# One wide matmul for two narrow ones in a channel mixer, and a new cost in the list schedule

## The chip, the cores and the metric

The kernel runs on one NeuronCore of a Trainium2 chip. The metric is the device time of one execution in microseconds (us); smaller is better.

## The reference

One block of a language model works on 256 tokens of 1024 features. It has a token mixer with three branches (block-sparse attention called NSA, an mLSTM, and cross attention to a memory), a gated merge, an output projection, and then a channel mixer. The channel mixer is the part that the change rewrites:

```python
x = x + rmsnorm(y @ w_out[l], g_post_mix[l])

h = rmsnorm(x, g_pre_ffn[l])
gu = h @ w_ffn_in[l]                       # [256, 1024] @ [1024, 5632]
gate, up = gu[..., :D_FF], gu[..., D_FF:]  # D_FF = 2816
x = x + rmsnorm((jax.nn.silu(gate) * up) @ w_ffn_down[l], g_post_ffn[l])
```

All values are float32.

## The kernel before

**Products in three parts.** TensorE multiplies float32r values here. So that the result is near float32, each float32 array is split into a high part (a ScalarE copy to float32r) and a low part (VectorE: the value less its high part); that is `split`. A product is then three matmuls into one accumulator: high x high, high x low, low x high. `mm3` issues the three, and `fmaj` does so for all eight feature tiles of 128.

**Units.** The weights come as 162 units of 128 x 1024 (512 KB), each by one DMA of SyncE's queue into one of four buffers `raw`. `unit` fetches one and splits it into `whi` (ScalarE) and `wlo` (VectorE), four buffers each.

**Two forms of a product.** `fmaj` and `fpair` keep a block of the weights stationary and move the activations: an accumulator [128 features, 256 tokens], matmuls 256 columns wide. `tmaj` keeps a block of the activations stationary and moves the weights: [128 tokens, 512 features], matmuls 512 wide. The merge gates, the queries and most of the input projection use the first form; the output projection, the first four feature tiles of the channel mixer (`gate0`, `up0`) and the down projection (`scaled`, "ffn_down") the second.

**The channel mixer.** `xh` and `xl` are the high and low part of the activations, feature-major [128, 8, 256]. For the feature tiles i = 4 to 21 a loop makes `fpair` (gate tile and up tile, one unit each, in the two halves of one bank of PSUM), multiplies the gate by 1/rms (`rfb`), applies silu on ScalarE, multiplies by the up half, and splits the result into `us`, the operand of the down projection. `ps_ds` chooses the bank: two of tag "d", then three of tag "s", in turn.

**The order of the work.** The kernel text only records instructions. `Plan.schedule` then makes a list schedule over all engines: every instruction has a cost (`Plan.cost`), latencies between engines are added, and on every engine the ready instruction that comes first in the program is issued. The result is a fixed order on each engine. For TensorE, `op.load` is a least distance between two matmuls (109 ns for float32r), and the cost is the columns at 2.4 per ns and 2 ns. A tag of a pool gets as many buffers as the first request for it says.

Of the kernel before, what the change touches and what calls it, by code (L numbers as in the profile page):

```python
# [18 lines left out]
S = 256          # tokens  # L19
D = 1024  # L20
KD = D // P      # feature tiles of the model dimension
# [11 lines left out]
# columns of w_in  # L33
C_Q, C_KV, C_G, C_ML, C_IF, C_O, C_QM, C_MG = 0, 1024, 2560, 2608, 4144, 4152, 4664, 5176

# columns of the array of constants
K_ID, K_TRI, K_RV, K_BM, K_M0, K_C1, K_MT, K_END = 0, 128, 256, 257, 261, 533, 549, 677
# columns of the array of gains and small weights
# [4 lines left out]
class View:  # L43
    """A part of a tile that has no place yet."""
# [54 lines left out]
    def region(self):  # L99
        """First and last partition, and the elements of a partition as bits."""  # L100
        t = self.tile
        key = repr(self.steps)
        if key not in t.regions:
            p = int(self.ix.flat[0]) // t.n
            bits = np.zeros(t.n, bool)
            bits[self.ix[0].ravel() % t.n] = True
            t.regions[key] = (p, p + self.shape[0], int.from_bytes(np.packbits(bits).tobytes(), "big"))
        return t.regions[key]


class Slot:
    """A tile of the plan: its place is chosen when its first instruction is issued."""
# [50 lines left out]
class Plan:  # L163
    """Records the instructions in program order, with what they read and write, and issues them
    in the order of a list schedule: on every engine the ready one that comes first in the
    program. Tiles of a tag get their buffers in program order."""
# [8 lines left out]
    @contextmanager  # L175
    def later(self, n):
        """The instructions inside come as if n places later in the program."""
        self.boost -= n
        yield
        self.boost += n  # L180
# [46 lines left out]
    @staticmethod  # L227
    def cost(op):
        n = op.outs[0].n if op.outs else 0
        views = op.outs + op.ins  # L230
        sources = [v for v in op.ins if not v.tile.psum and v.n > 1]
        wide = op.method in ("tensor_copy", "tensor_scalar") and not any(v.tile.psum for v in op.outs)
        op.port = op.eng == "POOL" and bool(op.ins) or op.eng == "DVE" and len(sources) > 1 - wide
        if op.eng == "SP":
            return math.prod(views[0].shape) * 4 / 360.0
        if op.eng == "PE":
            dtype = op.a[1].dtype
            op.load = 56.0 if dtype == BF16 else 109.0 if dtype == F32R or op.method == "transpose" else 214.0
            rate = 1.2 if op.method == "transpose" else 0.6 if dtype == F32 else 2.4
            return n / rate + 2  # L240
        n = max(v.n for v in views)
        psum = any(v.tile.psum for v in views)
        pointers = sum(v.n == 1 for v in op.ins)
        if op.eng == "ACT":
            return (50 if psum else 95) + 0.833 * n + 93 * ("accum_out" in op.kw or pointers > 0)
        if op.eng == "DVE":
            fast = not psum and op.method in ("tensor_copy", "tensor_scalar")
            return 67 + (0.52 if fast else 1.04) * n + 60 * pointers
        if op.method == "memset":
            return 40 + 0.8 * n  # L250
        if op.kw.get("op") == ALU.pow:
            return 300 + 165 * n
        if op.method == "tensor_copy":
            return 100 + 3.4 * n
        return 100 + 1.4 * n if op.method == "tensor_scalar" else 150 + 2.1 * n
# [9 lines left out]
    def schedule(self):  # L265
# [10 lines left out]
        def offer(op):  # L276
            """Makes op a candidate if its new tiles can have places; else it waits for the tag."""
            r = op.ready
            for t in op.tiles:
                if t.real is None:  # L280
                    tag = t.tag
                    if tag.next != t.seq or not tag.free:
                        tag.waiting.setdefault(t.seq, []).append(op)
                        return
                    r = max(r, tag.free[0][0])
            avail[op.eng].append((max(r, held(op)), op))

        def held(op):
            """A bank of PSUM serves one engine at a time, and so do the ports that GpSimd shares."""
            ends = [end + self.latency(o, op) for t in op.tiles if t.psum  # L290
                    for e, (o, end) in t.busy.items() if e != op.eng]
            if op.port:
                ends += [end for e, end in port.items() if e != op.eng]
            return max(ends, default=0.0)
# [91 lines left out]
def block_kernel(ctx, tc, order, xN, xT, memT, cst, vec, row, wg, w1, w2, W, out):  # L386
# [75 lines left out]
    def fmaj(out, xs, ks, wu, b0=0, first=True, last=True):  # L462
        """out [128 features, 256] += blocks of a unit (from b0) times the tiles ks of xs."""
        hi, lo = wu
        for i, k in enumerate(ks):
            b = slice((b0 + i) * P, (b0 + i + 1) * P)
            mm3(out, hi[:, b], lo[:, b], xs[0][:, k, :], xs[1][:, k, :],
                first and i == 0, last and i == len(ks) - 1)

    def fpair(xs, w, i, ps_new=ps_d):  # L470
        """[128, 2, 256]: the i-th pair of feature tiles of the weights w."""
        ps = ps_new([P, 2, S])
        for j in range(2):
            fmaj(ps[:, j, :], xs, range(KD), unit((w, 2 * i + j)))
        return ps

    def tmaj(xs, *key, n=4, ps_new=ps_d, into=None, last=0):
        """[128 tokens, 512] for both halves of the tokens, from n units of two feature tiles each; the
        last ones are used for the first half of the tokens before the second."""
# [29 lines left out]
    def warm_up(n):  # L509
        """Products of no use, that bring the tensor engine's clock up while it would wait."""  # L510
# [4 lines left out]
    def colsum(sq):  # L515
        """[128, 2]: per token, the sum of sq [128, 2, 256] over the partitions and the tiles."""
# [7 lines left out]
    def bcast(r, ps):  # L524
        """ps [128, 256]: the column r [128, 2] of the tokens, on every row."""
# [114 lines left out]
    msk = one.tile([P, 416], BF16, name="msk")          # m0 (272), c1 (16), mt (128)  # L640
# [56 lines left out]
    # running sums of logf, and i - sums  # L697
# [34 lines left out]
    # columns: selected keys 128-255, 0-127, compressed keys, window keys 0-127, 128-255  # L732
    kh = bigt("KK", 2, [P, NG, 528], F32R, "kh")
    kl = bigt("KK", 2, [P, NG, 528], F32R, "kl")
# [61 lines left out]
    for h2 in range(2):  # L796
        pvm = ps_v([P, 2, S], "pvm")
        ptm = [[work.tile([P, 2, S], F32R, tag=f"pT{i}", bufs=2, name="pTm") for i in range(2)] for _ in range(2)]
        for tb in range(2):
# [18 lines left out]
            pt = ps_t([P, 2, 2, P], "ptx")          # m tile, head, t  # L818
# [256 lines left out]
    def scaled(name, xs, n, g, z, scale, pre):  # L1075
        """z [128 tokens, 2, 1024]: the products with the units of a name times the gains g and, per token,
        pre; yields per half of the tokens 1/rms of the products times the root of scale."""
# [17 lines left out]
    xh = bigt("KK", 2, [P, KD, S], F32R, "xh")  # L1095
    xl = bigt("KK", 2, [P, KD, S], F32R, "xl")
# [34 lines left out]
    for tb in range(2):  # L1131
# [7 lines left out]
        split(us[0][:, 0, :, t], us[0][:, 1, :, t], pt)  # L1139
    for i in range(4, KF):  # L1140
        ps = fpair((xh, xl), "ffn_in", i, ps_ds)
        sl_ = work.tile([P, S], F32, tag="sq", bufs=3, name="silu")
        DVE.tensor_mul(sl_, ps[:, 0, :], rfb)
        ACT.activation(sl_, sl_, AF.Silu)
        DVE.tensor_mul(sl_, ps[:, 1, :], sl_)
        u = us[i // 4]
        split(u[:, 0, i % 4, :], u[:, 1, i % 4, :], sl_)
# [19 lines left out]
def _layout(inputs):  # L1167
# [10 lines left out]
    def blocks(w, cols, k0=0, k1=None):  # L1178
        """[128, k, cols] of the rows k0..k1 (tiles)."""
# [69 lines left out]
def _stream(units, order):  # L1249
    """The units in the order of their use."""  # L1250
# [27 lines left out]
```

## Time and the profile before

| | |
|---|---|
| median of 3 runs | 562.93 us (562.88 to 563.34) |
| span of the profiled execution, first to last instruction | 561.4 us |
| the median less that span | 1.5 us |
| TensorE matmuls (PE), busy | 551.9 us, 98% |
| TensorE weight loads (PEld), busy | 516.5 us, 92% |
| VectorE (DVE), busy | 404.5 us, 72% |
| ScalarE (ACT), busy | 334.2 us, 60% |
| mean DMA rate | 170 GB/s |

The page gives no separate total time for the profiled execution; its own time is the span and what lies around it. In the page's lines, a group such as `pd<-xh,whi` names the tile that is written, then the tiles that are read; "128x256" is partitions by elements of the moving operand; the numbers after the bar are the group's busy time in us, the mean ns of one instruction from start to end, and the engine's idle time before it. All instructions are recorded in one helper, so all stand at line 382, and groups are told apart by their tiles: in the channel mixer `pd` and `pss` are the banks of tag "d" and "s". A row of a timeline or of the chain begins with its start and its length in us. Matmuls overlap in the array, so the sum of their lengths is more than their share of the time.

### The profile page before, as it was taken

What the parts mean: (1) busy time and instruction counts of PE and PEld (TensorE: products, weight loads), DVE (VectorE), ACT (ScalarE), POOL (GpSimd) and SP (SyncE); (2) the same over time, 40 slices, a digit from 0 to 9 for tenths busy, and PEclk for the clock granted to TensorE, in tenths of its full rate; (3) what the DMA queues carried; (4) which work ended last, traced back from release to release, by engine and by line L of the source; (5) the groups of instructions that cost most, each with busy time, mean ns of one, the idle gap of its engine ahead of it and who ended that gap; (6) DMA issues with size and microseconds to landing.
All of it is one profiled execution on the core that took longest, in us unless ns stands there. A gap on an engine that the chain in (4) does not pass through costs nothing.

```text
span 561.4 us, 10304 instructions
## 1 busy us (share of the span) xinstructions
PE 551.9 (98%) x3964; PEld 516.5 (92%) x3964; DVE 404.5 (72%) x802; ACT 334.2 (60%) x658; POOL 36.0 (6%) x44
## 2 busy tenths in 40 slices
PE   8999999999999999999999999999999999999994
PEld 8899998998989999999999998878999999988883
DVE  4897398598897989987786877865565656654543
ACT  6775677566596858777697444774444444444430
POOL 1110000002002011302111000000000000000000
PEclk9999999999999999999999999999999999999998
DMA  7994327617345253434435655744555545556522
GB/s 246 356 350 154 113 86 228 205 56 238 129 121 180 76 178 124 135 119 160 151 117 158 216 189 188 257 156 123 177 189 183 182 175 179 186 185 191 189 71 75
DMA packets 29281, 95.28 MB, mean 170 GB/s; under 512 B 3376, under 2 KB 6704, under 8 KB 28976
## 3 DMA queue, kind: packets, MB, share of 16 engines
q1 hardware_dynamic: 29232, 94.63, 51.5%
q8 instruction: 31, 0.51, 0.4%
q14 instruction: 18, 0.15, 0.1%
HBM read 92.52 MB, written 1.05 MB: 167 GB/s over the span
## 4 chain that ended last, share of the span: by engine, by line
PE 92%; DMA 3%; ACT 2%; DVE 2%; issue 0%; SPq 0%; DVEq 0%; ACTq 0%
PE pd L382 46%; PE pss L382 23%; PE pnl L382 6%; PE sc L382 3%; PE pvn L382 3%; PE pmm L382 2%; PE ptn L382 2%; DMA memt<-in_memT 2%; PE ph L382 2%; ACT whi L382 1%; DMA raw<-in_W 1%; PE pw L382 1%; PE pn L382 1%; PE pgf L382 1%; PE psm L382 1%; PE pvm L382 1%
## 5 line engine op out<-in xcount | busy, mean ns | idle before, releaser
L382 DVE TENSOR_TENSOR wlo<-raw,whi 128x1024 fp32r<-128x1024 f32 (+1 forms) x161 | 195.4, 1217 | 102.1 <-ACT whi L382 100.7
L382 ACT ACTIVATE whi<-raw 128x1024 fp32r<-128x1024 f32 (+1 forms) x161 | 167.6, 1046 | 164.3 <-issue 72.3
L382 PE MATMUL pd<-hh,whi 128*128 128x256 f32 x416 | 119.7, 288 | 0.3 <-DVE vs L382 0.3
L382 PE MATMUL pd<-hh,wlo 128*128 128x256 f32 x416 | 119.7, 288 | 0.0
L382 PE MATMUL pd<-hl,whi 128*128 128x256 f32 x416 | 119.5, 287 | 0.0
L382 PEld LDWEIGHTS pd<-hh,whi 128*128 128x128 f32 x416 | 79.5, 191 | 0.8 <-DVE vs L382 0.7
L382 PEld LDWEIGHTS pd<-hl,whi 128*128 128x128 f32 x416 | 79.4, 191 | 0.1
L382 PEld LDWEIGHTS pd<-hh,wlo 128*128 128x128 f32 x416 | 79.4, 191 | 0.0
L382 PE MATMUL pss<-xh,wlo 128*128 128x256 f32 x160 | 45.4, 284 | 0.0
L382 PE MATMUL pss<-xl,whi 128*128 128x256 f32 x160 | 45.4, 284 | 0.0
L382 PE MATMUL pss<-xh,whi 128*128 128x256 f32 x160 | 45.4, 283 | 0.0
L382 PE MATMUL pss<-whi,u 128*128 128x512 f32 x132 | 42.4, 392 | 0.0
L382 PE MATMUL pd<-xh,whi 128*128 128x256 f32 x128 | 36.2, 283 | 0.0
L382 PE MATMUL pd<-xl,whi 128*128 128x256 f32 x128 | 36.2, 283 | 0.0
L382 PE MATMUL pd<-xh,wlo 128*128 128x256 f32 x128 | 36.2, 283 | 0.0
L382 PEld LDWEIGHTS pss<-xh,whi 128*128 128x128 f32 x160 | 30.7, 192 | 0.0
L382 PEld LDWEIGHTS pss<-xl,whi 128*128 128x128 f32 x160 | 30.7, 192 | 0.0
L382 PEld LDWEIGHTS pss<-xh,wlo 128*128 128x128 f32 x160 | 30.7, 192 | 0.0
L382 PEld LDWEIGHTS pss<-whi,u 128*128 128x128 f32 x132 | 24.8, 188 | 5.5
L382 ACT ACTIVATE pp<-sc,mx 128x128 f32<-128x128 f32 (+1 forms) x64 | 27.1, 439 | 0.4 <-DVE mx L382 0.3
L382 PE MATMUL pss<-wlo,u 128*128 128x512 f32 x66 | 25.9, 392 | 0.0
L382 DVE TENSOR_REDUCE mx<-sc 128x1 f32<-128x16 f32 (+2 forms) x96 | 22.6, 284 | 3.3 <-PE sc L382 3.0
(306 smaller groups left out, 1243.9 us busy)
## 6 DMA issues: line engine op xcount, KB each, us to landing
raw<-in_W SPq DMA_DIRECT2D x159, 512.0 KB, 3.4
w<-in_w SPq DMA_DIRECT2D x2, 1024.0 KB, 7.0
raw<-in_W SPq DMA_DIRECT2D x6, 256.0 KB, 5.6
xt<-in_xT SPq DMA_DIRECT2D x2, 512.0 KB, 7.6
x<-in_xN SPq DMA_DIRECT2D x2, 512.0 KB, 4.9
out<-z SPq DMA_DIRECT2D x8, 128.0 KB, 2.0
memt<-in_memT SPq DMA_DIRECT2D x6, 128.0 KB, 5.4
wgt<-in_wg SPq DMA_DIRECT2D x1, 512.0 KB, 6.3
```

The source lines that it names most:

```text
L382: op.ins_ = getattr(op.real, op.method)(*map(arg, op.a), **{k: arg(x) for k, x in op.kw.items()})
```

## The change

The high and low activations come to stand side by side in one tile, `xc` [128, 8, 2, 256]. A new function `fcat` multiplies a block of the high weights by both with one matmul 512 wide, into the two halves of a bank, and a block of the low weights by the high activations with one matmul 256 wide, into the first half. A unit thus takes 16 matmuls for 24, with the same number of columns, and a whole bank, where before a pair of units shared one. `joined` adds the two halves: ScalarE copies the second half to a work tile, VectorE adds the first. It asks for six buffers of tag "sq", which has been made with three. `kh` and `kl` of the attention, which had the buffers of `xh` and `xl` before, become the halves of one tile. And `Plan.cost` gives a float32r matmul 13 ns beside its columns instead of 2. The other lines of the diff only drop comments and docstrings; the core of it is:

```diff
-            return n / rate + 2
+            return n / rate + (13 if dtype == F32R and op.method != "transpose" else 2)
...
+    def fcat(xc, w, ps):
+        hi, lo = unit(w)
+        b = lambda k: slice(k * P, (k + 1) * P)
+        for k in range(KD - 1):
+            PE.matmul(ps, hi[:, b(k)], xc[:, k], start=k == 0, stop=False)
+        for k in range(KD):
+            PE.matmul(ps[:, 0, :], lo[:, b(k)], xc[:, k, 0], start=False, stop=False)
+        PE.matmul(ps, hi[:, b(KD - 1)], xc[:, KD - 1], start=False, stop=True)
+        return ps
...
-    kh = bigt("KK", 2, [P, NG, 528], F32R, "kh")
-    kl = bigt("KK", 2, [P, NG, 528], F32R, "kl")
+    kk_ = bigt("KK", 1, [P, 2, NG, 528], F32R, "kk")
+    kh, kl = kk_[:, 0], kk_[:, 1]
...
-    xh = bigt("KK", 2, [P, KD, S], F32R, "xh")
-    xl = bigt("KK", 2, [P, KD, S], F32R, "xl")
+    xc = bigt("KK", 1, [P, KD, 2, S], F32R, "xc")
+    xh, xl = xc[:, :, 0], xc[:, :, 1]
...
+    def joined(ps):
+        t = work.tile([P, S], F32, tag="sq", bufs=6, name="join")
+        ACT.activation(t, ps[:, 1, :], AF.Copy)
+        DVE.tensor_add(t, t, ps[:, 0, :])
+        return t
+
     for i in range(4, KF):
-        ps = fpair((xh, xl), "ffn_in", i, ps_ds)
-        sl_ = work.tile([P, S], F32, tag="sq", bufs=3, name="silu")
-        DVE.tensor_mul(sl_, ps[:, 0, :], rfb)
-        ACT.activation(sl_, sl_, AF.Silu)
-        DVE.tensor_mul(sl_, ps[:, 1, :], sl_)
+        gate = joined(fcat(xc, ("ffn_in", 2 * i), ps_ds([P, 2, S])))
+        DVE.tensor_mul(gate, gate, rfb)
+        ACT.activation(gate, gate, AF.Silu)
+        up = joined(fcat(xc, ("ffn_in", 2 * i + 1), ps_ds([P, 2, S])))
+        DVE.tensor_mul(up, gate, up)
         u = us[i // 4]
-        split(u[:, 0, i % 4, :], u[:, 1, i % 4, :], sl_)
+        split(u[:, 0, i % 4, :], u[:, 1, i % 4, :], up)
```

## The prediction

> **What bounds the kernel now.** I read the page's busy shares first, then the chain that ended last, then TensorE's waits, and then the trace of the channel mixer alone.
>
> ```profile
> span 561.4 us, 10304 instructions
> PE 551.9 (98%) x3964; PEld 516.5 (92%) x3964; DVE 404.5 (72%) x802; ACT 334.2 (60%) x658; POOL 36.0 (6%) x44
> ...
> PEclk9999999999999999999999999999999999999998
> ...
> PE 92%; DMA 3%; ACT 2%; DVE 2%; issue 0%; SPq 0%; DVEq 0%; ACTq 0%
> ...
> 20.00:300.00 280.00, 279.55 (x2148) 265.19 (x2147) 230.84 (x544) 200.39 (x464) 31.62 (x27) 1.00 0.49 160
> ...
> PE warm L382 <- POOL ones L382: 1.0, 1, 1.0
> ...
> PE pd L382 <- ACT xh L382: 0.2, 1, 0.2
> ```
>
> TensorE is the bound: it is busy for 98% of the span at full granted clock, the chain is 92% matmuls, and between 20 and 300 us (columns of the window row: length, then busy time of PE, PEld, DVE, ACT, POOL) it lacks 0.45 us. The six waits listed for it run from 1.0 to 0.2 us. So time is saved only by making TensorE's own instruction stream shorter, and lost by anything that makes it wait. Busy time cannot say how short, because the matmuls overlap in the pipeline; for that I need start-to-start times.
>
> The span is 561.4 us, and the median of the runs shown is 562.93, so 1.5 us lie around the span. I take these as unchanged and subtract from 562.93.
>
> **The removed and added matmuls.** The stage that is changed is 18 pairs of units, 36 units, each of 24 matmuls 256 wide:
>
> ```profile
> L382 PE MATMUL pss<-xh,whi 128*128 128x256 f32 x160 | 45.4, 283 | 0.0
> ...
> L382 PE MATMUL pd<-xh,whi 128*128 128x256 f32 x128 | 36.2, 283 | 0.0
> ```
>
> Two more groups of each count (the products with xl and with wlo) make (160 + 128) x 3 = 864 = 36 x 24. The 283 ns are start to end; the pace is in the chain, whose pieces give start, length and count:
>
> ```profile
> 395.73 11.52 PE pd L382 x96
> 407.25 17.28 PE pss L382 x144
> ...
> 493.65 31.73 PE pss L382 x138
> 543.50 5.44 PE pss L382 x24
> ```
>
> 11.52 us by 96 and 17.28 us by 144 are both 120.0 ns for a 256-wide matmul. The last two pieces are 512-wide ones of the down projection: 5.44 us by 24 is 226.7 ns, but 31.73 us by 138 is 229.9 ns. Twice the columns thus cost 107 to 110 ns more, not 120: about 13 ns belong to each matmul and not to its columns. Why the two paces differ shows where TensorE passes from narrow to wide matmuls:
>
> ```profile
> 342.35 0.40 PE L382 MATMUL pd<-whi,yh 128*128 128x512 f32 x1
> ...
> 344.19 0.39 PE L382 MATMUL pss<-whi,yl 128*128 128x512 f32 x1
> ...
> 493.49 0.39 PE L382 MATMUL pss<-whi,u 128*128 128x512 f32 x1
> ...
> 494.64 0.64 PE L382 MATMUL pss<-whi,u 128*128 128x512 f32 x2
> 495.11 0.39 PE L382 MATMUL pss<-wlo,u 128*128 128x512 f32 x1
> 495.34 0.39 PE L382 MATMUL pss<-whi,u 128*128 128x512 f32 x1
> ```
>
> The rows at 342.35 and 493.49 are the first wide matmul after a narrow run, those at 344.19 and 495.34 the ninth: eight take 1.84 us and 1.85 us, 230 and 231 ns each. The slowest pair within them takes 0.47 us (494.64 to 495.11), 235 ns each. A wide run starts slow and settles to 226.7 only later.
>
> `fcat` makes a unit of 7 wide, 8 narrow, 1 wide. Counted in the two programs' orders, TensorE has 288 matmuls fewer, 36 x 8, and the same columns. In the new order one unit's last wide matmul stands ahead of the next unit's seven, so a wide run is eight long and always follows a narrow run. I therefore take the entry price, 1.845 us for eight, and 8 x 0.120 = 0.960 for the narrow ones: 2.805 us against 24 x 0.120 = 2.880, 0.075 a unit, **2.7 us** for 36. The bounds are the settled pace (8 x 0.2267 + 0.960 = 2.774, 0.106 a unit, 3.8 us) and the slowest pair's pace throughout (8 x 0.235 + 0.960 = 2.840, 0.040 a unit, 1.4 us). A loss is excluded on TensorE: in no row does a wide matmul take as long as two narrow ones, 240 ns.
>
> The Trainium skill (TensorE: Matmul & The Clock Gate, Back-to-back issue gap) gives an isolated start-to-start time of N/2.4 + 2.5 ns, 109 and 216 ns here; by it the fixed part is 2.5 ns and the edit saves 0.7 us as an estimate from that page. The rows, 120 and 226.7, do not agree with it for these operands.
>
> **What is added on VectorE and ScalarE.** `joined` adds a ScalarE copy of 256 columns from PSUM and a VectorE add to each unit:
>
> ```profile
> 400.00:480.00 80.00, 80.00 (x669) 80.00 (x668) 49.29 (x70) 37.65 (x55) 0.00 (x0) 1.00 0.55 182
> ...
> L382 DVE TENSOR_TENSOR wlo<-raw,whi 128x1024 fp32r<-128x1024 f32 x28 | 34.3, 1225 | 26.9 <-ACT whi L382 26.9
> L382 DVE TENSOR_TENSOR u<-silu,u 128x256 fp32r<-128x256 f32 x14 | 5.9, 418 | 0.0
> L382 DVE TENSOR_TENSOR silu<-pss,rfb 128x256 f32<-128x256 f32 x8 | 3.4, 425 | 2.4 <-PE pss L382 2.4
> L382 ACT ACTIVATE whi<-raw 128x1024 fp32r<-128x1024 f32 x28 | 29.7, 1061 | 42.4 <-issue 42.4
> L382 ACT ACTIVATE silu<-silu 128x256 f32<-128x256 f32 x14 | 5.6, 400 | 0.0
> L382 ACT ACTIVATE pTm<-ptx 128x256 fp32r<-128x256 f32 x8 | 2.6, 383 | 0.0
> ```
>
> In this stage VectorE is busy for 49.3 of 80 us. Per pair it has two weight splits, two products and the split of u: 2 x 1.225 + 2 x 0.425 + 0.418 = 3.7 us of 5.76. Two adds at the price of the row with one operand in PSUM, 0.425, make 4.6 of 5.61 us. ScalarE has 2 x 1.061 + 2 x 0.400 = 2.9 us, and two copies at the 0.383 of the nearest copy out of PSUM make 3.7. Both stay under TensorE's time, so the price is nothing while the weights arrive early. What is queued behind the copy, which waits for its unit's last matmul, is ScalarE's weight copy (whi), and behind that VectorE's wlo. In the new order the copy of unit n stands ahead of whi of unit n+3: three units, 8.4 us, ahead of its use, while copy, whi and wlo take 0.38 + 1.06 + 1.23 = 2.7 us. If that cover were gone, each unit would wait for up to these 2.7 us.
>
> PSUM: a unit now takes a whole bank where a pair did. Five banks rotate (two of tag d, three of tag s), each is free again a copy and an add, 0.8 us, after its unit and wanted four units, 11 us, later: nothing. `bufs=6` in `joined` has no effect: the tag sq was made with three buffers, and a tag keeps its first number. A gate tile lives about one unit longer than an up tile; three buffers at one per 2.8 us hold 8.4 us: nothing. One KK tile for two: both halves are read until the last scores anyway, and the copies into xc wait for the same transposes: nothing. The weight stream must run 4% faster in the stage, and the DMA share there is 0.55: nothing. The tail after the last matmul is the same.
>
> **The new cost in the list schedule.** `cost` now gives 119.7 ns to a 256-wide float32r matmul, which is the 120.0 of the rows; before it paced them by 109. This reorders all engines from the start, not the channel mixer alone. SyncE's weight loads keep their order; the copies between the halves of kh and kl come two loads later, the loads of x a few loads earlier, all with the DMA far from full. ScalarE's 13 function-table loads stay 13. No operation is added there, so what changes is waits. To gain there is little: the 0.45 us of the first window row (waits hidden under a matmul's overlap may add to it). What can be lost lies in the NSA attention passes:
>
> ```profile
> 220.00:240.00 20.00, 20.00 (x172) 19.65 (x170) 19.55 (x52) 15.43 (x49) 4.98 (x4) 1.00 0.32 107
> ...
> 265.08 0.47 DVE L382 TENSOR_SCALAR pp<-pp,sm 128x128 f32<-128x128 f32 x2
> ...
> 265.62 0.27 PE L382 MATMUL ptn<-cs,pp 128*128 128x128 f32 x1
> ```
>
> VectorE is 98% busy for 20 us here, and a transpose starts 0.07 us after the probabilities it reads are ready (265.08 + 0.47 = 265.55). The plan had covered this chain with matmuls that it thought 9% shorter than they are, and still it is just in time. In the new order the matmuls between a pass's last scores and its first transpose come, at the measured paces, to 6.7 us on average over the 16 passes, and before to 8.1; the thinnest to 2.7, and before 2.9. So some transposes will now wait. Ends: 0.5 us gained, and 16 passes late by 0.6 us (9% of 8.1 is 0.7, less 0.07), 10 us lost. Most passes have filling left and TensorE was kept full before with covers as thin as 2.9 us, so I take the low end, a loss of **0.3 us**, an estimate.
>
> Sum: 562.93 - 2.7 + 0.3 = **560.5 us**; the span would be about 559.0.
>
> **Rivals.** First, the wide runs settle at once, at 226.7 ns: 562.93 - 3.8 = 559.1, with the order's part 558.8 to 559.4. The settled pieces speak for it, both entries quoted against it. Chance 0.12.
>
> Second, the order takes back what the width gives: the 16 passes late by 0.1 to 0.24 us each, 1.6 to 3.8 us. Then it ends within 0.2% of before, 561.8 to 564.0, which is about what a measurement of this kernel can tell from no change. The just-in-time transpose speaks for it; against it, that the new cost is the measured pace, so the filling is now chosen by true prices. Chance 0.15.
>
> Third, slower: the transposes of the NSA passes, between 110 and 295 us, wait for VectorE's pp for more than 0.24 us a pass. From there it decides: 16 x 0.24 = 3.8 us is the 2.7 gained and 0.2%, 1.1 us, more. At 0.4 us a pass it is 562.93 - 2.7 + 6.4 = 566.6. For it: VectorE at 98%, and a sixth of the cover gone. Against it: TensorE's waits in the profile before are nearly none with the cheaper, wrong price. Chance 0.09.
>
> Fourth, a wide matmul saves next to nothing where wide and narrow runs alternate: the slowest pair, 235 ns against 240 for two narrow ones, becomes the rule. The gain is then the lower bound, 5 ns x 288 = 1.4 us, and the time 561.5. By the Trainium skill's formula above (TensorE: Matmul & The Clock Gate) it would be 562.2. Chance 0.04, since 138 wide matmuls in a row averaged 229.9.
>
> **How the numbers follow.** My forecast has 0.60 and runs from 559.5 to 561.7: 2.5 to 2.9 us by the two entries' rows, and the order between 0.5 gained and 1.3 lost. Faster by over 0.2% (below 561.8): 0.60 + 0.12 + half of 0.04 = 0.74; within: 0.15 + 0.02 = 0.17; slower: 0.09. The range leaves out the third rival and the upper part of the second, and little below: 558.8 to 562.8.
>
> **What would show it.** Right: in the chain, pieces of 16 matmuls a unit at 2.77 to 2.82 us; a wide pace of 227 to 232 ns in the stage; no TensorE wait there; VectorE near 80% of its time in it; the stage shorter by 2.5 to 3 us and its start, near 390 us, within 1 us of before. Wrong: idle TensorE ahead of ptn released by VectorE's pp, the channel mixer starting later than before by more than the stage gains, or waits for whi or for PSUM in the mixer's units.

## The result, and the profile after

| | median, us | runs, us |
|---|---|---|
| before | 563.13 | 562.88 to 563.34 |
| after | 568.32 | 567.79 to 569.49 |

The changed kernel is slower: the ratio is 1.0091, with a 95% interval from 1.0076 to 1.0106. The forecast was 560.5 us, and its range ended at 562.8. The profiled execution of after took 568.65 us, with a span of 566.9, so 1.8 us lie around the span (1.5 before).

The page of after, its head and the shares of its chain:

```profile
span 566.9 us, 9841 instructions
PE 552.4 (97%) x3676; PEld 500.7 (88%) x3676; DVE 421.7 (74%) x838; ACT 349.1 (62%) x694; POOL 35.3 (6%) x44
...
PEclk9999999999999999999999999999999999999998
...
PE 83%; DVE 6%; ACT 6%; DMA 2%; issue 2%; SPq 0%; DVEq 0%; ACTq 0%
```

TensorE has the predicted 288 instructions fewer, and its clock is as before. Yet its busy time has grown by half a microsecond, and the chain has 9 points less of it; VectorE and ScalarE have taken its place. The clock and the DMA queues (mean 168 GB/s) offer no cause. To see where, I set the starts of the first matmul of each part side by side, in us from the start of the span:

| first matmul of | before | after | later by |
|---|---|---|---|
| scores of the first NSA pass (`sc`) | 111.29 | 112.63 | 1.34 |
| merge (`pnl`) | 296.11 | 303.17 | 7.06 |
| output projection | 342.35 | 349.04 | 6.69 |
| transposes of x (`ptx`) | 364.14 | 370.88 | 6.74 |
| channel mixer's loop (`rbc` of rf) | 388.49 | 397.05 | 8.56 |
| down projection | 493.49 | 498.94 | 5.45 |
| last matmul | 553.99 | 559.45 | 5.46 |

The loop that was rewritten is 3.1 us shorter. Everything that was not rewritten, ahead of it, is 8.6 us longer: 7.1 before the merge and 1.8 between `ptx` and `rbc`, less 0.3 in the merge.

**The channel mixer.** The chain of after; each row is start, length and count:

```profile
401.34 5.59 PE pd L382 x32
406.92 8.38 PE pss L382 x48
...
499.10 30.34 PE pd L382 x132
529.44 30.41 PE pss L382 x132
```

5.59 us by 32 matmuls of two units and 8.38 by 48 of three make 2.794 us a unit, where before it was 2.880: 0.086 by 36 is 3.1 us. The timeline of TensorE shows a unit from inside (start, length, kind, count):

```profile
403.97 1.77 PE L382 MATMUL pd<-xc,whi 128*128 128x512 f32 x7
405.57 1.12 PE L382 MATMUL pd<-xc,wlo 128*128 128x256 f32 x8
406.53 0.40 PE L382 MATMUL pd<-xc,whi 128*128 128x512 f32 x1
406.76 1.77 PE L382 MATMUL pss<-xc,whi 128*128 128x512 f32 x7
```

And a window of after, in the columns of the prediction's:

```profile
400.00:480.00 80.00, 80.00 (x461) 70.48 (x460) 63.58 (x100) 49.36 (x86) 0.00 (x0) 1.00 0.52 185
```

Seven wide ones take 1.60 us, 229 ns each, eight narrow ones 0.96, the last wide one 0.23. The down projection's two long pieces average 230 ns, as the long piece of before did; within each of them the first part runs at 232 ns and the last at 226.7 (more on this at the end). VectorE is busy for 63.6 of the window's 80 us and ScalarE for 49.4, and TensorE does not stop for them.

**The attention.** Windows of after (length, then busy time and count of PE, PEld, DVE, ACT, POOL; clock, DMA share, GB/s), and behind them the same of the kernel `width_only` (below), whose order up to here is that of before:

```profile
40.00:100.00 60.00, 59.21 (x447) 56.25 (x446) 43.37 (x91) 38.75 (x75) 2.69 (x2) 1.00 0.45 147
220.00:240.00 20.00, 19.18 (x156) 18.21 (x155) 16.95 (x47) 12.94 (x39) 5.16 (x4) 1.00 0.25 87
100.00:300.00 200.00, 197.45 (x1520) 184.81 (x1519) 164.68 (x413) 140.87 (x356) 23.16 (x19) 1.00 0.39 138
```

```profile
40.00:100.00 60.00, 60.00 (x455) 57.66 (x455) 43.93 (x92) 40.27 (x76) 1.49 (x2) 1.00 0.49 156
220.00:240.00 20.00, 20.00 (x170) 19.51 (x168) 19.50 (x51) 15.42 (x50) 4.98 (x4) 1.00 0.32 107
100.00:300.00 200.00, 199.56 (x1571) 189.68 (x1570) 168.06 (x419) 145.42 (x365) 26.81 (x20) 1.00 0.43 143
```

Count the matmuls, not the busy time. In the 200 us of NSA, after starts 51 fewer; at the mean pace of 200 / 1571 = 0.127 us these are some 6.5 us, an estimate, since the mix of widths in the two windows is not the same. TensorE's busy time shows only 2.1 of them, because a matmul is 283 ns long and the next can start 120 ns later: a wait of up to 160 ns vanishes under the one before. The weight loads' busy time drops by 4.9, and shows more. The Trainium skill (Perfetto Trace Analysis, Identifying the Most-Contended Engine) calls matmul busy time no good measure of how close a kernel is to its roofline, and would use the weight loads' busy share, beside the FLOPs, instead. It says nothing there of hidden waits; in these rows the weight loads' 4.9 us come nearer to the 6.5 than the matmuls' 2.1.

What one such wait is made of shows in the timeline of after, one NSA pass:

```profile
265.27 0.29 PE L382 MATMUL sc<-msk,identb 128*128 128x272 bf16 x1
265.40 1.23 DVE L382 TENSOR_TENSOR wlo<-raw,whi 128x1024 fp32r<-128x1024 f32 x1
...
266.67 1.52 DVE L382 TENSOR_REDUCE mx<-sc 128x1 f32<-128x16 f32 x9
...
267.33 0.27 ACT L382 ACTIVATE pc<-sc,mx 128x16 f32<-128x16 f32 x1 [2.38 <-DVE mx L382]
...
267.83 0.28 PE L382 MATMUL pd<-hh,whi 128*128 128x256 f32 x1
...
268.45 0.51 PE L382 MATMUL sc<-kk,qs 128*128 128x272 f32 x2 [0.34 <-ACT pp L382]
...
272.05 0.28 PE L382 MATMUL pd<-hh,wlo 128*128 128x256 f32 x1
...
272.34 0.28 DVE L382 TENSOR_SCALAR pp<-pp,sm 128x128 f32<-128x128 f32 x1
...
272.68 0.33 PE L382 MATMUL ptn<-cs,pp 128*128 128x128 f32 x1 [0.35 <-DVE pp L382]
```

The first scores are complete at 265.56, but VectorE has begun a weight subtraction of 1.23 us at 265.40, and their maxima come behind it, at 266.67. So ScalarE's exponentials begin at 267.33, 1.77 us after the scores (the 2.38 us in brackets are all of ScalarE's idle time before them), and the fourth group of scores, which needs one of the three `sc` banks back, starts 0.62 us after the matmul before it and not 0.12: half a microsecond lost, of which 0.34 shows as a wait. At 272.68 a transpose starts 0.63 us after its predecessor and 0.06 us after the probabilities that it reads are ready: another half. The same pass before:

```profile
259.83 0.29 PE L382 MATMUL sc<-msk,identb 128*128 128x272 bf16 x1
...
260.36 0.57 DVE L382 TENSOR_REDUCE mx<-sc 128x1 f32<-128x16 f32 x3
...
261.02 0.27 ACT L382 ACTIVATE pc<-sc,mx 128x16 f32<-128x16 f32 x1 [0.39 <-DVE mx L382]
...
262.53 1.21 DVE L382 TENSOR_TENSOR wlo<-raw,whi 128x1024 fp32r<-128x1024 f32 x1
```

There the maxima come first, 0.24 us after the scores, the exponentials 0.90 us after them, and the weight subtraction 2 us after the maxima. The maxima of after are thus 0.87 us later behind their scores. Both engines issue in the order in which the plan left them. TensorE's list of waits in after names five such partners (waits in us, times, the longest), none over 0.6 us in all:

```profile
PE pvn L382 <- DVE yT L382: 0.6, 1, 0.6
PE pvm L382 <- DVE ymemt L382: 0.4, 1, 0.4
PE pd L382 <- DVE wlo L382: 0.4, 2, 0.2
PE ptn L382 <- DVE pp L382: 0.4, 1, 0.4
PE sc L382 <- ACT pp L382: 0.3, 1, 0.3
```

**The gate's first stage.** Timelines of after, and of before:

```profile
370.88 1.32 PE L382 MATMUL ptx<-cs,x 128*128 128x128 f32 x8
...
371.53 1.06 ACT L382 ACTIVATE whi<-raw 128x1024 fp32r<-128x1024 f32 x1 [0.52 <-PE ptx L382]
...
372.50 1.05 ACT L382 ACTIVATE sq<-x 128x1024 f32<-128x1024 f32 x1
...
373.54 2.16 ACT L382 ACTIVATE xc<-ptx,vc 128x128 fp32r<-128x128 f32 x8
373.94 0.73 PE L382 MATMUL pd<-wq,xc 128*128 128x512 f32 x2 [1.74 <-ACT xc L382]
```

```profile
364.14 1.03 PE L382 MATMUL ptx<-cs,x 128*128 128x128 f32 x8
...
364.93 2.16 ACT L382 ACTIVATE xh<-ptx,vc 128x128 fp32r<-128x128 f32 x8
...
365.33 0.74 PE L382 MATMUL pd<-wq,xh 128*128 128x512 f32 x2 [0.16 <-ACT xh L382]
```

In after ScalarE takes up another weight copy (371.53) ahead of the copies into `xc`, and behind it the square of x (372.50), which before had begun ahead of the transposes, at 363.89. The next product starts 3.06 us after the start of the transposes instead of 1.19: the stage's 1.8 us in one wait.

### The profile page after: what moved, and what is told of

Its sections match the earlier page's. It is cut to its first block, busy times and chain, and to the rows that moved or that the text cites. A ratio compares the mean times of both kernels' runs of the same rounds, so it can differ in the third digit from the quotient of the medians.

```text
span 566.9 us, 9841 instructions
## 1 busy us (share of the span) xinstructions
PE 552.4 (97%) x3676; PEld 500.7 (88%) x3676; DVE 421.7 (74%) x838; ACT 349.1 (62%) x694; POOL 35.3 (6%) x44
## 4 chain that ended last, share of the span: by engine, by line
PE 83%; DVE 6%; ACT 6%; DMA 2%; issue 2%; SPq 0%; DVEq 0%; ACTq 0%
PE pd L382 41%; PE pss L382 23%; PE pnl L382 6%; PE pvn L382 2%; ACT pp L382 2%; PE sc L382 2%; PE pmm L382 2%; DVE wlo L382 2%; DMA memt<-in_memT 2%; PE ph L382 2%; PE ptn L382 1%; ACT whi L382 1%; ACT pc L382 1%; DVE mx L382 1%; DVE pp L382 1%
## 5 line engine op out<-in xcount | busy, mean ns | idle before, releaser
L382 PE MATMUL pss<-xc,whi 128*128 128x512 f32 x176 | 46.0, 394 | 0.0
L382 PEld LDWEIGHTS pss<-xc,whi 128*128 128x128 f32 x176 | 32.1, 189 | 5.5
L382 PE MATMUL pd<-xc,whi 128*128 128x512 f32 x112 | 29.2, 392 | 0.0
L382 PE MATMUL pss<-whi,u 128*128 128x512 f32 x88 | 27.6, 392 | 0.0
L382 PE MATMUL pd<-whi,u 128*128 128x512 f32 x88 | 27.5, 392 | 0.0
L382 PEld LDWEIGHTS pss<-xc,wlo 128*128 128x128 f32 x176 | 24.0, 190 | 1.7
L382 PE MATMUL pss<-xc,wlo 128*128 128x256 f32 x176 | 24.5, 282 | 0.0
L382 PEld LDWEIGHTS pd<-xc,whi 128*128 128x128 f32 x112 | 20.6, 189 | 3.6
L382 PE MATMUL sc<-kk,qs 128*128 128x272 f32 (+1 forms) x96 | 20.7, 309 | 1.0 <-ACT pp L382 0.3
L382 DVE TENSOR_SCALAR pp<-pp,sm 128x256 f32<-128x256 f32 (+1 forms) x72 | 20.5, 317 | 0.0
L382 PEld LDWEIGHTS pss<-whi,u 128*128 128x128 f32 x88 | 16.6, 188 | 3.7
```

What stands on the lines that cost most here:

```text
L382: op.ins_ = getattr(op.real, op.method)(*map(arg, op.a), **{k: arg(x) for k, x in op.kw.items()})
```

## The experiments

**Theory A**: the price in the list schedule does it. A plan that thinks a float32r matmul cheaper than it is puts more of them between a result on VectorE or ScalarE and its use; that surplus is slack, which covers whatever the plan does not foresee. With the 120 ns that a matmul really takes, results are planned to arrive just in time, and some arrive late. **Rival B**: no order but the one before suits; any reordering of this size loses as much. **Rival C**: the loss comes from `fcat` and `joined`, the banks and the KK tile.

**One half of the change each.** `width_only` is after with the old price, `cost_only` is before with the new one:

```diff
-            return n / rate + (13 if dtype == F32R and op.method != "transpose" else 2)
+            return n / rate + 2
```

> The change with the old cost of a float32r matmul (2 ns beside the columns). Up to the channel mixer the order on every engine is that of the kernel before. Theory (the wide matmuls save 3 us in the mixer, the new order costs the rest): 563.1 - 3.1 = 560.0 us, between 559.3 and 560.7; attention ends and the mixer starts as before, within 0.5 us. Rival (joined, the KK tile or the wide matmuls cost time outside their own stage): over 562.

> The kernel before with the new cost alone (13 ns). Up to the channel mixer the order on every engine is that of the changed kernel. Theory: the order carries the whole loss: attention ends 7 us later, the stage of gate0 and up0 is 1.8 us longer, so 563.1 + 8 to 9 = 571 to 572.5 us. Rival (the loss needs the wide matmuls, or one KK tile): within 1 us of 563.1.

`width_only` took 559.52 us (559.50 to 561.37), a ratio of 0.9938 [0.9916, 0.9959]; `cost_only` 573.32 (572.34 to 575.16), 1.0178 [1.0151, 1.0206]. The first merge product starts at 295.6 us and at 303.8; the mixer's loop takes 101.9 and 105.0. The first of these starts is in the row of the tile `pnl` in `width_only` (shortest, median and longest in ns, then the first and the last start):

```profile
L382 PE MATMUL pnl<-ymlt,whi x64: 280/283/287, 295.6 to 337.3; 128*128 128x256 f32 x64
```

The median of `cost_only` lies 0.8 us above the range expected. Two of its four runs took 574.28 and 575.16 us at a mean granted clock of 0.993 and 0.990; the other two, at 0.996 and 0.997, took 572.36 and 572.34. The width brings all of the gain, the price all of the loss, and the two add up: -3.6 and +10.2 make 6.6 on medians, or 5.6 with the two runs at the higher clock, where after measured 5.2, with intervals of 1.2 and 1.5 us either way on the two. Rival C is out. `width_only` beats both kernels.

**The price by stage.** `cost_late` has the old price up to the merge and the new one from there; `cost_early` the reverse.

```diff
-            return n / rate + (13 if dtype == F32R and op.method != "transpose" else 2)
+            return n / rate + (PACE[0] if dtype == F32R and op.method != "transpose" else 2)
...
+    PACE[0] = 13
```

The last line stands ahead of the merge; in `cost_early` it is `PACE[0] = 2`, and the price begins with 13.

> The change with the old cost for all that is recorded up to the gated merge and the new cost from there on. Attention's order is that of before but for 5 positions. Theory (7 us of the loss are attention's, 1.8 the stage of gate0 and up0): 560.0 to 562.0, depending on whether a third weight copy stands again ahead of the copies into xc on ScalarE. Rival (the new cost does its harm in the mixer's neighbourhood): 565 or more.

> The changed kernel with the list schedule's fixed part of a float32r matmul at 13 ns up to the gated merge and at 2 ns from there. Up to the merge its order on every engine is that of the changed kernel; the merge, the output projection, the gate's first stage and the channel mixer are planned as before. If the loss is made of two separate parts, attention (+7.1 us) and the gate's stage (+1.4 to +1.8), the time is 559.5 + 7.1 = 566.6 us, 565.8 to 567.3, the merge begins near 303.2 us and the stage from ptx1 to the mixer's first product is back at 24.4 us. If the gate's stage is disturbed by what the earlier order leaves behind (buffers, the load queue) and not by its own planning, the stage stays near 26 us and the time is that of the changed kernel, 568.3.

`cost_late`: 561.50 us (561.24 to 562.31), 0.9970 [0.9956, 0.9983]; from `ptx` to `rbc` it takes 25.75 us, `width_only` 24.34. `cost_early`: 567.50 us (566.37 to 568.15), 1.0084 [1.0068, 1.0101], 0.2 us above its range; its merge starts at 302.7, and the stage is back at 24.36, as its timeline shows (line 386 is the 382 of the others):

```profile
370.40 1.03 PE L386 MATMUL ptx<-cs,x 128*128 128x128 f32 x8
...
371.03 2.17 ACT L386 ACTIVATE xc<-ptx,vc 128x128 fp32r<-128x128 f32 x8
...
371.45 0.73 PE L386 MATMUL pd<-wq,xc 128*128 128x512 f32 x2
```

Here no weight copy stands between. So the gate's stage loses its 1.4 to 1.8 us by its own planning, and attention its 7 by its own.

**Other reorderings at the old price.** `w_dve` and `w_act` are `width_only` with 3 ns more for each VectorE or each ScalarE instruction in the plan: next to nothing as a price, but 1004 and 490 of the 2216 TensorE instructions ahead of the merge change places (1466 in after).

```diff
-            return 67 + (0.52 if fast else 1.04) * n + 60 * pointers
+            return 70 + (0.52 if fast else 1.04) * n + 60 * pointers
...
-            return (50 if psum else 95) + 0.833 * n + 93 * ("accum_out" in op.kw or pointers > 0)
+            return (53 if psum else 98) + 0.833 * n + 93 * ("accum_out" in op.kw or pointers > 0)
```

> The change with the old matmul cost, and VectorE's fixed cost in the plan 70 ns for 67: a small error put in that has nothing to do with TensorE's pace. 1004 of TensorE's 2216 positions up to the merge change (1466 with the new matmul cost). Theory A (what costs is the slack that the true matmul pace takes away): within 2 us of the 559.5 of the old order. Rival B (any reordering of a tuned order loses about so much): 564 to 568.

> The change with the old matmul cost, and ScalarE's fixed cost in the plan 3 ns higher; 490 of TensorE's 2216 positions up to the merge change. Theory A: within 2 us of 559.5. Rival B: 562 to 566.

`w_dve`: 561.39 us (560.68 to 561.76), 0.9972 [0.9960, 0.9983]. `w_act`: 559.72 us (559.01 to 560.72), 0.9940 [0.9924, 0.9957]. Reordering alone costs 0.2 to 1.9 us against `width_only`; there is something in B, but not 8 us.

**The dose.** `cost6` and `cost20` are after with 6 and 20 ns in place of 13.

```diff
-            return n / rate + (13 if dtype == F32R and op.method != "transpose" else 2)
+            return n / rate + (6 if dtype == F32R and op.method != "transpose" else 2)
```

> The changed kernel with 6 ns beside a float32r matmul's columns, not 13: the plan paces a 256-wide one by 112.7 ns, where the chip takes 120. Theory A: some of the slack is left, so between: 560.5 to 564.5. Rival B: anything, about 566.

> The changed kernel with 20 ns in place of 13: the plan paces a 256-wide matmul by 126.7 ns, more than the chip's 120. Theory A: still less slack, the results are awaited before the chip has them: 570 to 575. Rival B: anything, about 566, as likely below the changed kernel's 568.3 as above.

`cost6`: 564.82 us (564.22 to 566.53), 1.0035 [1.0022, 1.0048], a little above what was expected. `cost20`: 574.94 us of two runs (572.03 and 577.86), 1.0210 [1.0084, 1.0336]. The run of 577.86, which is the profiled one, had a mean granted clock of 0.989, the other 0.998. Windows of `cost20`, and of after, show where:

```profile
40.00:60.00 20.00, 17.16 (x104) 16.78 (x104) 9.80 (x17) 7.55 (x14) 0.19 (x1) 0.74 0.31 106
```

```profile
40.00:60.00 20.00, 19.66 (x156) 19.09 (x155) 11.96 (x23) 11.46 (x19) 0.20 (x1) 1.00 0.43 152
```

At a granted clock of 0.74 TensorE has 104 matmuls in these 20 us, where after has 156. So only the 572.0 is to be compared, and it is one run. With 2, 6, 13 and 20 ns the time is then 559.5, 564.8, 568.3 and 572.0: it rises all the way. The first 4 ns cost 5.3 us and the next 7 only 3.5; this may mean that part of it is not slack but the particular order, which is not shown.

**Slack given back in another way.** `lat_more` and `lat_300` keep the 13 ns and add 150 and 300 ns to the plan's latency behind each ScalarE and VectorE instruction (502 and 488 in `lat_300`); `w_lat` adds 150 at the old price.

```diff
-    LAT = {"PE": 257.0, "ACT": 202.0, "DVE": 188.0, "POOL": 75.0, "SP": 980.0}
+    LAT = {"PE": 257.0, "ACT": 352.0, "DVE": 338.0, "POOL": 75.0, "SP": 980.0}
```

> The changed kernel with 150 ns more in the plan's latency from ScalarE and from VectorE to any other engine; the matmul cost stays 13. Theory A (with the true matmul pace the plan leaves TensorE no slack against chains that it thinks too short; slack given back by hand helps): attention ends 3 to 7 us earlier than in the changed kernel, 561 to 565 us. Rival B (any reordering of an order that was tuned with the old cost loses some us, whatever its reason): 566 to 571, no better than the changed kernel.

> The changed kernel with the new cost of 13 ns and 300 ns more latency behind every ScalarE and VectorE instruction in the plan (150 ns gave 561.8 us). If the missing slack is the cause, the rest of the loss comes back, 559.0 to 561.5 us, with the merge beginning at 296 to 298 us. If 150 ns had already bought all that latency can buy, 561.5 to 563.5. If the gain of 150 ns was the luck of one order, it falls back towards 565 to 568.

> The changed kernel with the schedule's old cost of a matmul (2 ns) and, besides, 150 ns more latency behind every ScalarE and VectorE instruction in the plan: slack from both sources. Some 1260 of 2216 TensorE positions ahead of the merge move against the order of before. If planned slack is what TensorE lacks, and the old order still lacks some (8.2 us of its time between 40 and 305 us are waits), this gains or holds: 556.5 to 560.0 us. If the old order is already at the point where more slack is of no use, it is 559.5 to 561.5. If any reordering of this size costs what the new cost's did, 565 to 569.

`lat_more`: 561.84 us (561.37 to 564.24), 0.9986 [0.9972, 1.0000]. `lat_300`: 561.49 us (561.19 to 565.71), 0.9995 [0.9974, 1.0016]. `w_lat`: 559.91 us (559.45 to 560.58), 0.9947 [0.9932, 0.9962]. With the new price in place, latency alone brings back 6.5 of the 8.8 us that the price costs on top of the width, and twice the latency 0.4 more, which the intervals do not tell from nothing; the median of `lat_300` lies on the border of the first two ranges expected. At the old price more slack gains nothing. So lack of slack explains most of the loss, and slack saturates.

The same seen in the orders, for the span that the prediction looked at: TensorE's own work between a pass's last scores and its first transpose, mean of the 16 passes, with every instruction at 13.3 ns and 1/2.4 ns a column (which gives 120.0 and 226.6 ns; at this single price the prediction's 8.1 and 6.7 us are 7.65 and 6.36). Beside it stands the time that the passes take, from the first scores to the merge, in the profiled run:

| kernel | price, ns | latency added, ns | cover, us | passes, us | merge starts, us | median, us |
|---|---|---|---|---|---|---|
| `w_lat` | 2 | 150 | 9.14 | 184.2 | 295.5 | 559.9 |
| `w_act` | 2 | 0 | 7.95 | 184.6 | 296.5 | 559.7 |
| `lat_300` | 13 | 300 | 7.82 | 184.8 | 297.2 | 561.5 |
| `w_dve` | 2 | 0 | 7.78 | 186.0 | 297.0 | 561.4 |
| `width_only` | 2 | 0 | 7.65 | 184.7 | 295.6 | 559.5 |
| `cost6` | 6 | 0 | 7.42 | 187.5 | 298.8 | 564.8 |
| `lat_more` | 13 | 150 | 7.12 | 185.9 | 298.8 | 561.8 |
| after | 13 | 0 | 6.36 | 190.5 | 303.2 | 568.3 |
| `cost20` | 20 | 0 | 5.81 | 192.7 | 312.2 | 574.9 |

With 7.6 us of cover and more, the passes take at most 1.3 us more than in `width_only`, and the cover no longer decides; at 7.1 to 7.4 they take 1.2 and 2.8 us more, at 6.4 it is 5.8, and at 5.8 it is 8.0. Within the middle pair the kernel with less cover loses less, so cover is not all that counts. The start of the merge holds also what came ahead of the passes. In `cost20` it is 16.6 us late, but 8.6 of these are there at the first scores, after the stretch at the low clock; the run at the higher clock is 5.8 us shorter. In `lat_more` it is 3.2 us late, and 2.1 of these are there at the first scores; this profiled run took 563.5 us, where the median is 561.8. `cost6` starts the merge as late, with 2.8 of its 3.2 us lost in the passes, and loses 1.5 us again in the gate's stage.

## Why the prediction was wrong

**The bound.** Right: TensorE's own stream sets the time, and "lost by anything that makes it wait" is what happened. But I measured the room for loss by busy time, after saying that busy time cannot show it.

**The matmuls.** Right, and a little low: 2.7 us forecast at the entry price, 3.1 measured, within its bounds of 1.4 and 3.8. A unit takes 2.79 us, the wide pace in it is 229 ns. Against the Trainium skill (TensorE: Matmul & The Clock Gate, Back-to-back issue gap), by which the edit would have saved 0.7 us as an estimate, the trace decides: 3.1. The first rival, that wide runs settle at once, fell with the 229 ns, and the fourth, that they save next to nothing, with the 3.1 us. The reason given for the entry price, "a wide run starts slow and settles to 226.7 only later", does not hold in general. It fits the output projection (231 ns for the first six, then 226.7), but in the down projection of before the pace falls to 226.8 ns after 72 matmuls and is back at 232.6 after 60 more (523.83 us), with no narrow matmul between. So the price was right and its reason was not, and that the size came out so near is in part luck.

**VectorE and ScalarE in the mixer, PSUM, `sq`, KK, the weight stream.** Right: nothing. TensorE has no wait of note in the loop, and VectorE's load in it is the 80% foretold.

**The new cost in the list schedule.** This step failed: "I take the low end, a loss of 0.3 us". The runs show a loss of 8.8 us in its place (568.3 against 559.5 in `width_only`, medians); in the profiled runs it is 7.6 up to the merge (303.2 against 295.6) and 1.8 in the gate's stage, less 0.3 between. Both ends of that term had been named, 0.5 gained and 10 lost, and so had its mechanism; the size was taken from the wrong side. Three things were read wrongly. First, "most passes have filling left": 6.7 against 8.1 us was the very number that decides, and at the single price of the table seven of the sixteen passes had under 4 us left, where before two had. Second, "the filling is now chosen by true prices" was counted as a reason for safety, when the false price was what paid for all else that the plan has wrong. Third, the search for victims went no further than the transposes and the NSA passes. The banks of `sc`, `pvn` and `pvm`, the maxima behind a weight subtraction, and the gate's first stage lose too. The new order showed them, but I weighed in it only DMAs and function tables, not what now stands ahead of a waiting consumer on VectorE and ScalarE.

**The rivals.** The third had the place, the sign and nearly the price: at 0.4 us a pass it gave 566.6. Measured is 568.3. Against `width_only` the first scores start 1.8 us later (112.6 against 110.8), the passes themselves take 5.8 us more, 0.36 on each of the 16, and the gate's stage 1.8. So the price per pass was near, and what lies outside the passes makes the rest. But the rival put the whole price down to transposes that wait for `pp`; in the one pass shown the wait for an `sc` bank costs as much, so that the sizes agree is in part luck. Its 0.09 was too little; the reason held against it, that TensorE had nearly no waits with the cheaper price, was a reason for it.

**What stays open.** `lat_300` still lies 2.0 us above `width_only`. In its profiled run 1.6 us are lost by the first scores (112.4 against 110.8) and next to nothing in the passes, so the slack given back has mended the passes, and most of what is left arises ahead of them. `w_dve` lies 1.9 us above, 1.3 of them in the passes, at a like cover. Whether these are the residue of B or of waits that cover alone does not describe, these runs don't tell.

## What to carry to other kernels

When a planner orders the instructions, a cost in it is not only a measurement but also a safety margin: before making one truer, see which other errors it has been paying for, and give that slack back where it belongs, as latency behind the engines that deliver. A change to a global price is a change to every stage; judge it by itself, apart from the edit that prompted it. And where matmuls overlap, count how many start in a window: busy time hid two thirds of the loss in the NSA passes.

## What the runs showed of the hardware that was not expected

The pace of 512-wide float32r matmuls goes up and down without a narrow one between them. Counted in the trace, the down projection of after has 264 in a row: 72 start 232.4 ns apart on average (from 498.94 us), the next 60 226.8 (from 515.67), the next 78 232.6 (from 529.28) and the rest 226.9 (from 547.42), all at a granted clock of 1.00. In before it is the same at 493.49, 510.21, 523.83 and 541.97 us. What sets the pace is not shown.

A single VectorE instruction of 1.23 us in front of a reduction makes the maxima 0.87 us later behind their scores than before, and costs TensorE half a microsecond a long way on. The Trainium skill (PSUM — Partial Sum Buffer, Engine vs sequencer instructions) says that the queues of ScalarE and VectorE are strictly first in, first out, and the rows at 265.40 and 371.53 agree: what is ready waits there for what stands ahead of it.
